# Gated linear attention: the short products of a head pair laid side by side in the array instead of padded with zeros

## The chip, the cores and the metric

One NeuronCore of a Trainium2 chip runs the whole program. The metric is the device time of one execution in microseconds (us). "PE" is TensorE, whose matmuls and weight loads ("PEld") the profile records apart; "DVE", "ACT" and "POOL" are the vector, scalar and GpSimd engines; "SP" issues most of the DMAs.

## The reference, cut to what matters

The program is one layer of a decoder trunk over 2048 tokens: an input projection, three token mixers in parallel (MLA, RWKV-7 and chunked gated linear attention, GLA), gates, and an output projection. The change touches GLA alone. It has 4 heads, keys of 64 and values of 128 channels, and for a chunk of tokens it computes, per head,

```python
def step(state, inp):
    q_t, k_t, v_t, b_t = inp                      # b: running sum of log decays in the chunk
    diff = b_t[:, :, None] - b_t[:, None, :]
    dec = jnp.exp(jnp.where(causal, diff, -jnp.inf))
    att = jnp.einsum('bihd,bjhd,bijhd->bhij', q_t, k_t, dec)
    o = (jnp.einsum('bhij,bjhv->bihv', att, v_t)
         + jnp.einsum('bihk,bhkv->bihv', q_t * jnp.exp(b_t), state))
    b_last = b_t[:, -1]
    state = (state * jnp.exp(b_last)[..., None]
             + jnp.einsum('bjhk,bjhv->bhkv', k_t * jnp.exp(b_last[:, None] - b_t), v_t))
    return state, o
```

## The kernel before

The phases follow each other: RWKV (with many of the projections), MLA, GLA, merge. PE is kept busy in RWKV and GLA by projections whose results are needed later. In GLA these are the gate columns: class `Gates` issues 108 units, each 8 groups of three 512-column matmuls (lines 133 to 135, output tile `psd`), with weights that SP loads as `w_raw`, ACT rounds to `w_hi` (line 118) and POOL completes to `w_lo` (line 119).

GLA works on 16 chunks of 128 tokens, numbered `g`. Four heads make two pairs, `p`; the two heads of a pair lie in partitions 0 to 63 and 64 to 127 of the same tiles. For a chunk there are three steps:

- `prepare(g)`: for each of six levels (64, 32, 16, 8, 4, 2 tokens) it makes a tile `qk` that holds decayed keys at the even halves of a level's blocks and decayed queries at the odd halves. DVE subtracts (line 1059, tile `e`), ACT takes the exponential, DVE multiplies the queries (line 1063, `qk<-e,q`) and POOL the keys. Line 1072 makes the queries of the last level, line 1073 the queries `qe` that meet the state. A query tile has two copies, one per head, and in each copy the other head's partitions are zero; so DVE works on 64 partitions at a time, twice. The zeros are written once, in the memsets of line 981.
- `scores(g)`: the products of queries and keys, per pair. The stationary operand is 128 partitions (both heads) by 64 or 32 tokens, the moving operand holds the two zero-padded copies side by side, and all go to one PSUM tile `psc` per pair: one 64-token product, two of 32 tokens from the second level, sixteen 32x32 blocks from the next four levels, and four from the plain keys `kx`. That is 23 products a pair, 46 a chunk, all on line 1086. DVE masks and adds them (lines 1099, 1101), POOL and ACT place the result in `a` (tile `ga`).
- `result(g)`: per pair and head, `qe` times the state (line 1117, `pso<-gs,qk`), plus `a` times the values (line 1120, `pso<-vt,ga`); then keys times values for the new state (line 1112, `pso<-vt,kt`), as one 128x256 product of which only the two diagonal blocks are used, and DVE updates the state (line 1124, tile `gs`).

All operands are fp32 here, and the profile records each such product as two LDWEIGHTS and two MATMULs. "128\*32" in a row is the size of the array's tile that the product uses, rows by columns.

Each engine runs its instructions in a fixed order. The program is written as one stream, and a scheduler interleaves it with its own estimates of durations; `ga.behind` also keeps a step's first product behind a given number of gate units. `ga.until` sets how many units are written between the steps. An engine that waits holds everything behind it.

Of the kernel before, what the change touches and what calls it, by code (L numbers as in the profile page):

```python
# [847 lines left out]
AHEAD = 1.5  # L848
# [98 lines left out]
def phase_gla(k, more, a_up, y_dram, x, w_gate, pre):  # L947
# [3 lines left out]
    with ExitStack() as st:  # L951
# [23 lines left out]

        QK = []
        for i in range(2):
            ts_ = [qkp[i].tile([128, 2, 2, 128], F32, name=f"qk{i}{n}") for n in range(len(LEVELS) + 1)]
            ts_.insert(-1, qkp[i].tile([128, 2, 2, 2, 128], F32, name=f"q{i}"))
            for n, t in enumerate(reversed(ts_)):  # L980
                (nc.vector, nc.gpsimd)[n % 2].memset(t, 0.0)
            QK.append(ts_)
        state, A = [], []
        for p in range(2):
            s_ = per.tile([128, 256], F32, name=f"gs{p}")
            nc.vector.memset(s_, 0.0)
            state.append(s_)
            for i in range(2):
                a = per.tile([128, 2, 128], F32, name=f"ga{p}{i}")
                nc.gpsimd.memset(a, 0.0)  # L990
                A.append(a)
        glam = k.c("glam", 192).rearrange("p (l t) -> p l t", t=32).unsqueeze(2).broadcast_to([128, 6, 2, 32])
        own = k.c("own32", 4).unsqueeze(2).broadcast_to([128, 4, 32])
# [50 lines left out]
        def prepare(g, kx, z, b, eb, kt, vt):  # L1044
# [5 lines left out]
            for hd, hs in heads:  # L1050
                nc.scalar.dma_start(out=q[hs, hd], in_=more[0:2, hs, g * 128:g * 128 + 128].rearrange("n p t -> p n t"))
            for s, o in zip(LEVELS, lv):
# [9 lines left out]
                for hd, hs in heads:  # L1062
                    nc.vector.tensor_tensor(out=v4(o[:, hd])[hs, :, 1, :], in0=ev[hs, :, 1, :],
                                            in1=v4(q[:, hd])[hs, :, 1, :], op=ALU.mult)
                nc.gpsimd.tensor_tensor(out=v4(o[:, 0])[:, :, 0, :], in0=ev[:, :, 0, :], in1=v4(kx)[:, :, 0, :],
# [5 lines left out]
            for hd, hs in heads:  # L1071
                nc.vector.tensor_tensor(out=odd(q1[:, hd])[hs], in0=e1[hs], in1=odd(q[:, hd])[hs], op=ALU.mult)
                nc.vector.tensor_tensor(out=qe[hs, hd], in0=eb[hs], in1=q[hs, hd], op=ALU.mult)

        def scores(g, kx, z, b, eb, kt, vt):
            c = g % 2
            *lv, q01, qe = QK[c]
            for p in range(2):
                a = A[2 * p + c]


                pc = ps_c[p].tile([128, 512], F32, name=f"psc{p}")
                pl = pc[:, 0:384].rearrange("p (l h t) -> p l h t", l=6, h=2)
                p64 = pc[0:64, 384:512].rearrange("p (h t) -> p h t", h=2)
                p32 = pc[:, 384:448].rearrange("p (h t) -> p h t", h=2)
                mm = lambda o, l, r: nc.tensor.matmul(o, lhsT=l, rhs=r, start=True, stop=True)
                m = mm(p64, lv[0][:, 0, p, 0:64], lv[0][:, :, p, 64:128])
                ga.behind(m, ga.done - AHEAD + p)
                mm(p32[96:128], lv[1][:, 0, p, 0:32], lv[1][:, :, p, 32:64])
                mm(p32[64:96], lv[1][:, 0, p, 64:96], lv[1][:, :, p, 96:128])  # L1090
                for i in range(5):
                    for j in range(4):
                        gs = slice(32 * j, 32 * j + 32)
                        if i < 4:
                            mm(pl[gs, i], lv[2 + i][:, 0, p, gs], lv[2 + i][:, :, p, gs])
                        else:
                            mm(pl[gs, 4:6], kx[:, c, p, gs], q01[:, :, :, p, gs])
                bm = t2.tile([128, 6, 2, 32], F32, name="bm")
                nc.vector.tensor_tensor(out=bm, in0=pl, in1=glam, op=ALU.mult)
# [479 lines left out]
```

## Time and profile before

| | |
|---|---|
| median of 3 runs | 3022.0 us (3018.12 to 3023.85) |
| the profiled execution | 3010.5 us, span 3008.7 us |
| PE busy | 2908.3 us, 97% of the span, 17728 matmul records |
| DVE / ACT / POOL busy | 59% / 50% / 49% |
| granted TensorE clock, mean | 0.989 |
| short products of GLA on PE | between 1853 and 2485 us of the span |

A PE that shows 97% busy is the engine to watch, but its records overlap: a matmul's duration covers the time until its result is out, while the next one starts earlier. What a product costs is therefore read from the distance between starts in the timeline. "Idle before, releaser" tells what an engine waited for.

### The profile page before, as it was taken

The page shows a single profiled execution, that of the slowest core. Times are in us where ns is not written, and L with a number is a line of the kernel's source. Part 1 is how long each engine was busy: PE and PEld are TensorE (multiplying, and loading weights), DVE is VectorE, ACT ScalarE, POOL GpSimd, SP SyncE. Part 2 cuts the span into 40 slices and gives each one's busy share as a digit, 9 for nine tenths or more (in the row PEclk, how much of TensorE's full clock was granted, in tenths as well). Part 3 has the DMA queues.
Part 4 walks back from the last instruction along what each step waited for, and adds up shares of the span by engine and source line. Part 5 has one row for each costly group of instructions (what it writes and reads, how often), then busy time and mean ns, then how long its engine had stood idle before and what let it go on. Part 6 is the DMA issues. An engine that isn't in the chain of part 4 may idle for free. (4 is left out here: it accounts for less than half of the span.)

```text
span 3008.7 us, 52742 instructions
## 1 busy us (share of the span) xinstructions
PE 2908.3 (97%) x17728; PEld 2395.9 (80%) x17728; DVE 1761.0 (59%) x4677; ACT 1503.9 (50%) x3463; POOL 1474.7 (49%) x1945
## 2 busy tenths in 40 slices
PE   7998999999999999999999999999999999999998
PEld 6776777777777878789999887788788888778887
DVE  3558675667746544388888886744324312975443
ACT  4444434454444436577877775554334434554221
POOL 4644544454444435555544555776334424575322
PEclk9999999999999999999999999999999999999999
DMA  4333323323233334300000014444223226866422
GB/s 135 105 100 103 90 85 101 93 77 86 78 106 86 106 112 144 113 20 22 19 20 16 15 62 148 148 143 136 92 96 101 92 91 203 288 201 212 137 97 78
DMA packets 285184, 312.67 MB, mean 104 GB/s; under 512 B 77920, under 2 KB 234608, under 8 KB 284912
## 3 DMA queue, kind: packets, MB, share of 16 engines
q1 hardware_dynamic: 259088, 278.76, 29.3%
q10 hardware_dynamic: 25824, 30.54, 3.1%
q8 instruction: 140, 2.29, 0.3%
q14 instruction: 132, 1.08, 0.1%
HBM read 233.16 MB, written 76.02 MB: 103 GB/s over the span
## 5 line engine op out<-in xcount | busy, mean ns | idle before, releaser
L119 POOL TENSOR_TENSOR w_lo<-w_raw,w_hi 128x256 fp32r<-128x256 f32 x848 | 645.0, 768 | 818.9 <-ACT w_hi L118 770.6
L133 PE MATMUL psd<-hh,w_hi 128*128 128x512 f32 x1952 | 795.1, 408 | 10.7 <-ACT w_hi L118 4.2
L135 PE MATMUL psd<-hh,w_lo 128*128 128x512 f32 x1952 | 788.4, 406 | 9.2 <-POOL w_lo L119 8.7
L134 PE MATMUL psd<-hl,w_hi 128*128 128x512 f32 x1952 | 778.3, 399 | 0.0
L118 ACT CAST w_hi<-w_raw 128x256 fp32r<-128x256 f32 x848 | 336.4, 404 | 501.8 <-PE psd L134 281.9
L135 PEld LDWEIGHTS psd<-hh,w_lo 128*128 128x128 f32 x1952 | 371.4, 190 | 95.5 <-POOL w_lo L119 17.9
L133 PEld LDWEIGHTS psd<-hh,w_hi 128*128 128x128 f32 x1952 | 371.2, 190 | 91.7 <-issue 8.9
L134 PEld LDWEIGHTS psd<-hl,w_hi 128*128 128x128 f32 x1952 | 371.1, 190 | 74.8 <-issue 1.2
L1286 POOL TENSOR_SCALAR P<-P,nm 128x1024 f32<-128x1024 f32 (+2 forms) x192 | 166.1, 875 | 192.5 <-DVE nm L1283 144.6
L1306 DVE TENSOR_TENSOR tl<-pst,th 128x512 fp32r<-128x512 f32 (+2 forms) x352 | 193.4, 562 | 33.6 <-ACT th L1305 32.0
L1305 ACT CAST th<-pst 128x512 fp32r<-128x512 f32 (+2 forms) x352 | 165.2, 488 | 81.6 <-PE pst L1301 42.5
L1278 ACT ACTIVATE P<-P,nm 128x1024 f32<-128x1024 f32 (+2 forms) x192 | 172.3, 901 | 14.8 <-DVE nm L1274 14.5
L1264 DVE TENSOR_SCALAR_CACHE_REDUCE P<-pss 128x512 f32<-128x512 f32 (+3 forms) x288 | 168.2, 593 | 13.1 <-PE pss L135 9.5
L1301 PE MATMUL pst<-cs,P 128*128 128x128 f32 x1088 | 166.0, 274 | 0.0
L1323 PE MATMUL pso<-th,v 128*128 128x256 f32 x576 | 150.9, 284 | 2.6 <-DVE yo L1331 2.6
L1323 PE MATMUL pso<-tl,v 128*64 128x256 f32 x576 | 139.9, 282 | 0.7 <-DVE tl L1306 0.7
L1301 PEld LDWEIGHTS pst<-cs,P 128*128 128x128 f32 x1088 | 125.6, 141 | 9.1 <-DVE tl L1306 0.4
L133 PE MATMUL pss<-kh,qh 128*128 128x512 f32 (+2 forms) x320 | 128.7, 402 | 0.6 <-DVE mx L1268 0.2
L119 POOL TENSOR_TENSOR wb_lo<-wb_raw,wb_hi 128x256 fp32r<-128x256 f32 x96 | 87.8, 921 | 80.6 <-ACT wb_hi L118 65.4
L1323 PEld LDWEIGHTS pso<-th,v 128*128 128x128 f32 x576 | 108.8, 189 | 11.8 <-DVE yo L1331 2.8
L135 PE MATMUL pss<-kh,ql 128*128 128x512 f32 (+2 forms) x320 | 116.4, 365 | 0.6 <-POOL ql L1244 0.6
L134 PE MATMUL pss<-kl,qh 128*128 128x512 f32 (+2 forms) x320 | 116.3, 364 | 0.0
(403 smaller groups left out, 5925.2 us busy)
## 6 DMA issues: line engine op xcount, KB each, us to landing
w_raw<-in_w_gate_dram SPq DMA_DIRECT2D x448, 128.0 KB, 2.2
pre<-plain SPq DMA_DIRECT2D x144, 256.0 KB, 2.3
w_raw<-in_w_rwkv_dram SPq DMA_DIRECT2D x208, 128.0 KB, 2.2
w_raw<-in_w_more_dram SPq DMA_DIRECT2D x192, 128.0 KB, 2.2
h_g<-pre SPq DMA_DIRECT2D x48, 512.0 KB, 4.4
h_x<-in_x_dram SPq DMA_DIRECT2D x44, 512.0 KB, 4.5
more<-plain SPq DMA_DIRECT2D x48, 256.0 KB, 2.7
wb_raw<-in_w_br_dram ACTq DMA_DIRECT2D x96, 128.0 KB, 3.5
```

What stands on the lines that cost most here:

```text
L118: nc.scalar.copy(hi, src)
L119: (sub or nc.gpsimd).tensor_tensor(out=lo, in0=src, in1=hi.bitcast(F32), op=ALU.subtract)
L133: mm(out, lhsT=lhs[0], rhs=rhs[0], start=start, stop=False)
L134: mm(out, lhsT=lhs[0], rhs=rhs[1], start=False, stop=False)
L135: m = mm(out, lhsT=lhs[1], rhs=rhs[0], start=False, stop=stop)
L1264: nc.vector.tensor_scalar(out=pt[:, c0:c0 + f], in0=s_[:, 0:f], scalar1=-MLA_SCALE, scalar2=3e38, op0=ALU.mult, op1=ALU.min, accum_out=mx[ ...
L1278: nc.scalar.activation(out=pt[:, cw], in_=pt[:, cw], func=AF.Exp, bias=nm[:, 0:1], scale=-1.0, accum_out=nm[:, 1 + n:2 + n])
L1286: nc.gpsimd.tensor_scalar(out=pt[:, cw], in0=pt[:, cw], scalar1=nm[:, 1:2], scalar2=1.0, op0=ALU.mult, op1=ALU.mult)
L1301: nc.tensor.transpose(tp[:, kl, qt, :], P[qt][:, kt * 128:(kt + 1) * 128], k.ident)
L1305: nc.scalar.copy(flat(th)[:, r], flat(tp)[:, r])
L1306: nc.vector.tensor_tensor(out=flat(tl)[:, r], in0=flat(tp)[:, r], in1=flat(th)[:, r].bitcast(F32), op=ALU.subtract)
L1323: nc.tensor.matmul(d_, lhsT=l_, rhs=r_, start=kt == 0 and j == 0, stop=last and kl == 1 and j == 1)
```

## The change

The zero-padded copies go. A query tile has one copy for both heads, `qk` is [128, 2, 128] instead of [128, 2, 2, 128], and DVE multiplies 128 partitions at once. In the scores each product is made per head, with 64 rows of the array each: the first head's in rows 0 to 63, the second's in rows 64 to 127, and each head has a PSUM bank of its own, `psc[hd]`, that now holds both pairs. So there are 92 products a chunk, and they stand in one run; masks and copies are made per head over both pairs. The products with the state are made per head with 64 rows as well, into `po[0]` and `po[1]`. The product for the new state is made per head with 64 columns of the array and all 128 rows; it goes to the second half of `po[0]`, and the state holds 128 instead of 256 columns. The memsets of the zeros go, except those of one query tile per buffer. The queries come in one DMA a chunk instead of two.

```diff
@@ phase_gla
-            ts_ = [qkp[i].tile([128, 2, 2, 128], F32, name=f"qk{i}{n}") for n in range(len(LEVELS) + 1)]
-            ts_.insert(-1, qkp[i].tile([128, 2, 2, 2, 128], F32, name=f"q{i}"))
-            for n, t in enumerate(reversed(ts_)):
-                (nc.vector, nc.gpsimd)[n % 2].memset(t, 0.0)
+            ts_ = [qkp[i].tile([128, 2, 128], F32, name=f"qk{i}{n}") for n in range(len(LEVELS) + 1)]
+            ts_.insert(-1, qkp[i].tile([128, 2, 2, 128], F32, name=f"q{i}"))
+            (nc.vector, nc.gpsimd)[i].memset(ts_[-2][:, 1], 0.0)
...
@@ prepare
-            for hd, hs in heads:
-                nc.scalar.dma_start(out=q[hs, hd], in_=more[0:2, hs, g * 128:g * 128 + 128].rearrange("n p t -> p n t"))
+            nc.scalar.dma_start(out=q, in_=more[0:2, :, g * 128:g * 128 + 128].rearrange("n p t -> p n t"))
...
-                for hd, hs in heads:
-                    nc.vector.tensor_tensor(out=v4(o[:, hd])[hs, :, 1, :], in0=ev[hs, :, 1, :],
-                                            in1=v4(q[:, hd])[hs, :, 1, :], op=ALU.mult)
+                nc.vector.tensor_tensor(out=v4(o)[:, :, 1, :], in0=ev[:, :, 1, :], in1=v4(q)[:, :, 1, :], op=ALU.mult)
...
-            for hd, hs in heads:
-                nc.vector.tensor_tensor(out=odd(q1[:, hd])[hs], in0=e1[hs], in1=odd(q[:, hd])[hs], op=ALU.mult)
-                nc.vector.tensor_tensor(out=qe[hs, hd], in0=eb[hs], in1=q[hs, hd], op=ALU.mult)
+            nc.vector.tensor_tensor(out=odd(q1), in0=e1, in1=odd(q), op=ALU.mult)
+            nc.vector.tensor_tensor(out=qe, in0=eb, in1=q, op=ALU.mult)
@@ scores
+            pc = [ps_c[hd].tile([128, 2, 256], F32, name=f"psc{hd}") for hd in range(2)]
+            def mm(at, out, l, r):
+                for hd, hs in heads:
+                    m = nc.tensor.matmul(out(pc[hd]), lhsT=l[hs], rhs=r[hs], start=True, stop=True)
+                    if at and hd == 0:
+                        ga.behind(m, ga.done - AHEAD)
             for p in range(2):
...
-                m = mm(p64, lv[0][:, 0, p, 0:64], lv[0][:, :, p, 64:128])
-                ga.behind(m, ga.done - AHEAD + p)
+                mm(p == 0, lambda o: o[0:64, p, 192:256], lv[0][:, p, 0:64], lv[0][:, p, 64:128])
...
-                            mm(pl[gs, i], lv[2 + i][:, 0, p, gs], lv[2 + i][:, :, p, gs])
+                            mm(False, lambda o: o[gs, p, 32 * i:32 * i + 32], lv[2 + i][:, p, gs], lv[2 + i][:, p, gs])
...
@@ result
+            po = [ps_o.tile([128, 512], F32, name="pso") for _ in range(2)]
+            a = A[c]
             for p in range(2):
-                for hd in range(2):
-                    m = nc.tensor.matmul(po[:, hd], lhsT=qe[:, hd, p], rhs=state[p][:, hd * 128:hd * 128 + 128], start=True, stop=False)
...
-                    nc.tensor.matmul(po[:, hd], lhsT=a[:, hd], rhs=vt[p][:, c, hd], start=False, stop=True)
-                nc.scalar.copy(osb[:, c, 2 * p:2 * p + 2], po)
-                pd_ = ps_o.tile([128, 256], F32, name="pso")
-                mm(pd_, kt[:, c, p], flat(vt[p][:, c]))
+                for hd, hs in heads:
+                    m = nc.tensor.matmul(po[hd][:, ps], lhsT=qe[hs, p], rhs=state[p][hs], start=True, stop=False)
...
+                for hd, hs in heads:
+                    nc.tensor.matmul(po[hd][:, ps], lhsT=a[:, hd, p], rhs=vt[p][:, c, hd], start=False, stop=True)
+            for p in range(2):
+                pd_ = po[0][:, 256 + 128 * p:384 + 128 * p]
+                for hd, hs in heads:
+                    nc.tensor.matmul(pd_[hs], lhsT=kt[:, c, p, hs], rhs=vt[p][:, c, hd], start=True, stop=True)
                 nc.vector.scalar_tensor_tensor(out=state[p], in0=state[p], scalar=eb[:, c, p, 127:128], in1=pd_,
                                                op0=ALU.mult, op1=ALU.add)
+            for hd in range(2):
+                nc.scalar.copy(osb[:, c, hd:4:2], po[hd][:, 0:256].rearrange("p (q t) -> p q t", q=2))
```

In the changed kernel the score products are on line 1080, the products with the state on 1115, `a` times values on 1119, and the new state's products on 1123. Three places show what the scheduler makes of it; a row is the line, the operation, output and inputs, and the output's partitions by columns ("x2": twice in a row).

On PE, the last chunk's `result` for the first pair, before (`psd` rows are gate products, on all of the array):

```order
L135 MATMUL psd_29709<-hh_25590,w_lo 128x512
L1117 MATMUL pso<-gs_22355,qk_22345 128x128
L1120 MATMUL pso<-vt_28327,ga_22359 128x128
L1117 MATMUL pso<-gs_22355,qk_22345 128x128
L1120 MATMUL pso<-vt_28327,ga_22359 128x128
L1112 MATMUL pso<-vt_28327,kt 128x256
L133 MATMUL psd_29819<-hh_23214,w_hi 128x512
```

The same place after the change, where both pairs' results now stand in one run:

```order
L135 MATMUL psd_30251<-hh_25773,w_lo 128x512
L1115 MATMUL pso<-gs_22341,qk_22338 128x128 x2
L1119 MATMUL pso<-vt_28720,ga_22347 128x128 x2
L1115 MATMUL pso<-gs_22343,qk_22338 128x128 x2
L1119 MATMUL pso<-vt_28721,ga_22347 128x128 x2
L1123 MATMUL pso<-vt_28720,kt 64x128 x2
L133 MATMUL psd_30361<-hh_23266,w_hi 128x512
```

Before, every product in this stretch uses all 128 rows and columns of the array; after, it goes from 128x128 to 64 rows, back, to 64 rows, back, to 64 columns and back to the gates, and the second pair's products for the state stand apart, 21 gate products later.

On PE, in the middle of the phase, where a block of the gates' input is turned, the score products of a chunk are interleaved with gate products. Before:

```order
L1086 MATMUL psc_26211<-qk_22343 32x64 x4
L133 MATMUL psd_26035<-hh_25584,w_hi 128x512
L1086 MATMUL psc_26211<-qk_22344 32x64
L133 MATMUL psd_26155<-hh_23222,w_hi 128x512
L134 MATMUL psd_26155<-hl_23223,w_hi 128x512
L1086 MATMUL psc_26211<-qk_22344 32x64 x3
```

After:

```order
L1080 MATMUL psc_26430<-qk_22336 32x32
L1080 MATMUL psc_26429<-qk_22336 32x32
L133 MATMUL psd_26373<-hh_23278,w_hi 128x512
L134 MATMUL psd_26373<-hl_23279,w_hi 128x512
L1080 MATMUL psc_26430<-qk_22336 32x32
L1080 MATMUL psc_26429<-qk_22336 32x32
```

Such places are more frequent now: counted over the whole phase, the score products stand in 36 unbroken runs before and in 53 after.

On DVE, near the end of MLA, the zeros of the first buffer before:

```order
L1268 ISA mx 128x1
L981 MEMSET qk_22329 128x512
L981 MEMSET qk_22328 128x512
L981 MEMSET qk_22326 128x512
L981 MEMSET qk_22324 128x512
L1331 TENSOR_TENSOR yo<-pso,yl 64x256
L1306 TENSOR_TENSOR tl<-pst,th 128x512
```

And after:

```order
L1270 ISA mx 128x1
L979 MEMSET q_22330 128x256
L1276 TENSOR_REDUCE nm<-mx 128x1
L1333 TENSOR_TENSOR yo<-pso,yl 64x256
L1308 TENSOR_TENSOR tl<-pst,th 128x512
L202 TENSOR_SCALAR h_x<-h_x,rs 128x1024
```

Four memsets of 512 columns have become one of 256 ahead of MLA's own work.

More of the change, by code (lines that the diff above doesn't have):

```diff
@@ L984, in phase_gla @@
         for p in range(2):
-            s_ = per.tile([128, 256], F32, name=f"gs{p}")
+            s_ = per.tile([128, 128], F32, name=f"gs{p}")
             nc.vector.memset(s_, 0.0)
             state.append(s_)
[L988 to L993, printed above, removed]
+        for i in range(2):
+            a = per.tile([128, 2, 2, 128], F32, name=f"ga{i}")
+            nc.gpsimd.memset(a, 0.0)
+            A.append(a)
+        glam = k.c("glam", 192).rearrange("p (l t) -> p l t", t=32).unsqueeze(1).broadcast_to([128, 2, 6, 32])
+        own = k.c("own32", 4).unsqueeze(1).unsqueeze(3).broadcast_to([128, 2, 4, 32])
         flat = lambda a: a.rearrange("p a b -> p (a b)")
@@ L1061, in prepare @@
                 nc.scalar.activation(out=e, in_=e, func=AF.Exp, scale=1.0 / 16)
[L1062 to L1065 removed]
+                nc.vector.tensor_tensor(out=v4(o)[:, :, 1, :], in0=ev[:, :, 1, :], in1=v4(q)[:, :, 1, :], op=ALU.mult)
+                nc.gpsimd.tensor_tensor(out=v4(o)[:, :, 0, :], in0=ev[:, :, 0, :], in1=v4(kx)[:, :, 0, :],
                                         op=ALU.mult)
@@ L1111, in result @@
             qe = QK[c][-1]
-            mm = lambda o, l, r: nc.tensor.matmul(o, lhsT=l, rhs=r, start=True, stop=True)
+            po = [ps_o.tile([128, 512], F32, name="pso") for _ in range(2)]
+            a = A[c]
             for p in range(2):
-                a = A[2 * p + c]
-                po = ps_o.tile([128, 2, 128], F32, name="pso")
-                for hd in range(2):
-                    m = nc.tensor.matmul(po[:, hd], lhsT=qe[:, hd, p], rhs=state[p][:, hd * 128:hd * 128 + 128], start=True, stop=False)
-                    if hd == 0:
-                        ga.behind(m, ga.done - AHEAD + p)
-                    nc.tensor.matmul(po[:, hd], lhsT=a[:, hd], rhs=vt[p][:, c, hd], start=False, stop=True)
-                nc.scalar.copy(osb[:, c, 2 * p:2 * p + 2], po)
-                pd_ = ps_o.tile([128, 256], F32, name="pso")
-                mm(pd_, kt[:, c, p], flat(vt[p][:, c]))
+                ps = slice(128 * p, 128 * p + 128)
+                for hd, hs in heads:
+                    m = nc.tensor.matmul(po[hd][:, ps], lhsT=qe[hs, p], rhs=state[p][hs], start=True, stop=False)
+                    if hd == p == 0:
+                        ga.behind(m, ga.done - AHEAD)
+                for hd, hs in heads:
[4 more added lines that the diff above has]
+                    nc.tensor.matmul(pd_[hs], lhsT=kt[:, c, p, hs], rhs=vt[p][:, c, hd], start=True, stop=True)
                 nc.vector.scalar_tensor_tensor(out=state[p], in0=state[p], scalar=eb[:, c, p, 127:128], in1=pd_,
                                                op0=ALU.mult, op1=ALU.add)
+            for hd in range(2):
+                nc.scalar.copy(osb[:, c, hd:4:2], po[hd][:, 0:256].rearrange("p (q t) -> p q t", q=2))
         def finish(B, osb):
```

29 lines of the change are left out of this document (12 added, 17 removed).

## The prediction

> **What bounds the kernel now.** I read the page's first part first (PE is busy nearly all of the span), then the stretches of GLA, then what PE waited for, then the timeline of PE at one chunk. In the stretches each engine's figure is its busy time:
>
> ```profile
> 1780.00:1800.00 20.00, 17.40 (x118) 16.01 (x117) 17.40 (x47) 14.06 (x31) 12.52 (x15) 0.91 0.47 163
> 1850.00:1880.00 30.00, 25.43 (x190) 19.40 (x188) 26.89 (x54) 16.68 (x45) 22.68 (x41) 0.89 0.33 108
> 1890.00:1910.00 20.00, 16.05 (x79) 12.74 (x79) 19.40 (x43) 11.63 (x32) 16.09 (x31) 0.91 0.40 138
> 2200.00:2460.00 260.00, 260.00 (x1781) 212.64 (x1781) 84.01 (x197) 95.75 (x241) 106.09 (x169) 1.00 0.28 93
> ```
>
> The columns are PE, PEld, DVE, ACT, POOL, then the granted clock. From 2200 to 2460 PE never pauses and DVE, ACT and POOL are busy a third of the time: there, time is PE's starts alone, and work taken from the others is worth nothing. Around 1790 and from 1850 to 1910 it is different: PE pauses, DVE is nearly full, and the clock is below 1. What PE waited for between 1780 and 1910 (total, times, longest):
>
> ```profile
> PE pst L1040 <- ACT kt L1041: 3.0, 1, 3.0
> PE psc L1086 <- DVE qk L1063: 2.9, 4, 1.2
> PE pso L1323 <- DVE yo L1331: 2.6, 1, 2.6
> PE pso L1117 <- DVE qk L1073: 1.7, 1, 1.7
> PE pso L1112 <- DVE gs L1124: 0.8, 1, 0.8
> ```
>
> So two prices decide: what the short products cost on PE in 16 chunks, and how much of these pauses at the start goes.
>
> **Score products, per chunk.** The last chunk's scores stand in one run; the starts are in the first column:
>
> ```profile
> 2453.47 0.39 PE L135 MATMUL psd<-hh,w_lo 128*128 128x512 f32 x1
> 2453.79 1.06 PE L1086 MATMUL psc<-qk 128*64 128x128 f32 x36
> 2454.64 0.28 PE L1086 MATMUL psc<-q,kx 128*32 128x128 f32 x2
> ...
> 2455.06 1.06 PE L1086 MATMUL psc<-qk 128*64 128x128 f32 x36
> ...
> 2456.32 0.50 PE L133 MATMUL psd<-hh,w_hi 128*128 128x512 f32 x1
> 2456.66 0.40 PE L134 MATMUL psd<-hl,w_hi 128*128 128x512 f32 x1
> ```
>
> 2.53 us for 46 products, and a frame: the gate product ahead holds PE 0.32 us and the one behind 0.34, where 0.23 is the usual distance (2478.01 to 2478.24 below). Together 2.73 us. Two other stretches give the parts:
>
> ```profile
> 1880.69 0.38 PE L1086 MATMUL psc<-q,kx 128*32 128x128 f32 x4
> 1881.00 0.49 PE L1117 MATMUL pso<-gs,qk 128*128 128x128 f32 x2
> 1881.32 0.39 PE L1120 MATMUL pso<-vt,ga 128*128 128x128 f32 x2
> 1881.55 0.39 PE L1117 MATMUL pso<-gs,qk 128*128 128x128 f32 x2
> ...
> 1882.42 0.43 PE L1086 MATMUL psc<-qk 128*64 128x128 f32 x2
> 1882.79 0.70 PE L1112 MATMUL pso<-vt,kt 128*128 128x256 f32 x2
> ```
>
> A 128x128 product in a steady row costs 0.22 us (1881.32 to 1881.55), but 0.32 directly behind a tile of another size (1881.00): 0.10 more, to load weights. The 64-column product costs 0.37 until another size follows: a record lasts some 0.28 (0.39 less the 0.11 between the two records of a product), so its second record starts 0.43 - 0.28 = 0.15 behind its first, 0.05 late, and some 0.20 more pass before another size may start. So of the 0.85 us to the first `kx` product, 0.49 is left for 34 records on four column tiles: 14 ns a record, 29 ns a product. Where nothing holds them, records start closer: these rows count score records in flight within 16, 37, 96 and 117 ns (PE, then PEld), and after 37 ns four matmuls run, after 96 ns eight loads are out:
>
> ```profile
> 1883.40:1883.42 0.02, 0.00 (x1) 0.00 (x1) 0.00 (x0) 0.00 (x0) 1.00 0.00 0
> 1883.40:1883.44 0.04, 0.02 (x4) 0.02 (x4) 0.00 (x0) 0.00 (x0) 1.00 0.00 0
> 1883.40:1883.50 0.10, 0.08 (x5) 0.08 (x8) 0.00 (x0) 0.00 (x0) 1.00 0.08 11
> ```
>
> That is three starts in 21 ns, 7 ns each. After the change each record streams half the columns on one of eight tiles. I take 7 ns, the row with nothing in the way; the other end is the 14 ns of now. The row-wise halving has a price that the RWKV phase shows, where 64\*64 and 128\*64 products (64 columns moved) alternate, and where the second kind stands alone:
>
> ```profile
> 374.74 0.33 PE L547 MATMUL psu<-uv,mr 128*64 128x64 f32 x2
> 375.00 0.33 PE L515 MATMUL psq<-uv,ma 64*64 64x64 f32 x2
> 375.25 0.33 PE L547 MATMUL psu<-uv,mr 128*64 128x64 f32 x2
> 217.32 0.68 PE L547 MATMUL psu<-uv,mr 128*64 128x64 f32 x8
> 217.93 0.71 PE L575 MATMUL psz<-uv,bkt 128*128 128x128 f32 x4
> ```
>
> Alternating, a product (two records) takes 0.26 us. Eight records alone take 0.61, of which entering and leaving is some 0.14: 0.12 a product. So a change of rows alone, with the columns kept, costs 0.14 us.
>
> After, per pair: the 64-token products of both heads 0.26 (the rows above, the second head's some 0.01 behind the first's); then 88 records (44 products) x 7 ns = 0.62, plus 0.15 until another size may follow: 0.77. Twice 1.03 and the frame of 0.20: 2.26 against 2.73. **Sixteen chunks: -7.5 us.** At 14 ns it would be +12.
>
> **Products of the result, per chunk.** Steady, before:
>
> ```profile
> 2478.01 0.39 PE L135 MATMUL psd<-hh,w_lo 128*128 128x512 f32 x1
> 2478.24 0.38 PE L1117 MATMUL pso<-gs,qk 128*128 128x128 f32 x2
> ...
> 2479.12 0.60 PE L1112 MATMUL pso<-vt,kt 128*128 128x256 f32 x2
> 2479.37 0.59 PE L133 MATMUL psd<-hh,w_hi 128*128 128x512 f32 x1
> 2479.80 0.40 PE L134 MATMUL psd<-hl,w_hi 128*128 128x512 f32 x1
> ```
>
> No size changes here. Four products take 0.88; the last one and the first gate product 0.68, less 0.23 for the gate product itself, 0.45. So 1.33 a pair, 2.66 a chunk. After: entering costs 0.09. The two 64-row products with the state run together: the second records 0.21 behind the first (0.11, and 0.10 for a load of 128 columns), 0.01 for the second head, then 0.20 until another size may follow, 0.42. The two with `a`: records 0.21, 0.11 and 0.11 apart, then 0.20, 0.64 in place of 0.44. Both again: 0.42 + 0.64. The state's pair in 64 columns: 0.37, and the gate product behind 0.11 more. Then, 21 gate products later, 0.09 + 0.37 + 0.11. Sum 3.26 against 2.66: the halved streams are paid back by six changes of size. **Sixteen chunks: +9.7 us** (if the row change were free, -3).
>
> [...]
>
> **Broken runs.** 53 runs of score products instead of 36. Each has the frame of 0.20 and the 0.15 at its end: 17 x 0.33 = 5.6, and a few state products that the scheduler set apart in the first chunks, 4 x 0.33. **+7 us.** PE in all: **+9.2 us.**
>
> **The start.** DVE's zeros stand ahead of what MLA waits for:
>
> ```profile
> 1785.97 2.11 DVE L981 MEMSET qk<- 128x512 f32 x4
> 1788.00 0.35 DVE L1331 TENSOR_TENSOR yo<-pso,yl 64x256 f32<-64x256 f32 x1
> 1788.41 0.38 PE L1323 MATMUL pso<-th,v 128*128 128x256 f32 x1 [2.60 <-DVE yo L1331]
> ```
>
> One memset of half the width, 0.27 us, replaces these: **-1.8 us** of 2.6 (0 if another wait is next, as `tl` behind `yo` on DVE may be). Then DVE between 1850 and 1910:
>
> ```profile
> L1063 DVE TENSOR_TENSOR qk<-e,q 64x128 f32<-64x128 f32 x46 | 21.1, 458 | 0.7
> L1059 DVE TENSOR_TENSOR e<-b 128x128 f32<-128x128 f32 x24 | 11.1, 500 | 0.2
> L1073 DVE TENSOR_TENSOR qk<-eb,q 64x256 f32<-64x256 f32 x8 | 5.3, 661 | 0.1
> ```
>
> Lines 1063 and 1073 keep their columns and halve their count. At 500 ns, the row of the same form on 128 partitions, 23 take 11.5 us, and 4 take 2.6: 12 us less in 60 that DVE all but fills. The other four waits of the list are 8.4 us and all end with DVE or with ACT behind it. The first of them come when only some 4 us are saved, so I take **-6 us** (bounds 0 and -8.4). The clock stood at 0.91, 0.89 and 0.91 over 20, 30 and 20 us, 6.9 us lost, in and just behind the pauses; half of it: **-3.4 us** (bounds 0 and -6.9). The start: -11.2.
>
> **At nothing.** The state update on half the columns, fewer POOL instructions for `ga`, one DMA of queries instead of two and the copies per head lie beside a PE that is full (2200 to 2460); without that cover they would be worth at most what DVE saves. A wait is added: the second pair's product for the state follows DVE's update of the first, since both lie in `po[0]`. Behind it wait gate products; 21 of them, 4.8 us, stand in between, so it costs nothing except in the first chunks, up to 2 us. Masks now begin only after both pairs' products, but 72 or more gate products, 16 us, follow.
>
> **Sum.** +9.2 - 11.2 = -2.0 us. The profiled execution took 3010.5 us (span 3008.7), so 3008.5; it stands 11.5 below the median of the runs, 3022.0, and against that I say 3020. A measurement of this kernel tells 0.2%, some 6 us, from no change.
>
> **Rivals.**
> - *Only the start counts* (faster): all of the pauses and of the clock's loss go, 17.9 instead of 11.2: 3013. DVE's 12 us speak for it; against it, that PE's order sets the GLA steps earlier where DVE is expected to be faster, and waits anew.
> - *The change of rows is free* (faster): result products -3 instead of +9.7, so 3007. The alternating rows at 374.74 speak against it; no row has 64 rows with 128 columns. Decides if 64-row products start 0.22 us behind a gate product's start. [...]
> - *Issue bounds the scores* (slower): a product cannot be sent faster than the 29 ns of now, so twice the products take twice as long: 44 x 29 = 1.28 instead of 0.62, twice a chunk, +21: 3041. For it, no row shows more than a burst at 7 ns; against it, at 29 ns four tiles are full with their columns, which explains it without any limit. It decides above some 11 ns a record. [...]
> - *The second head does not run beside the first* (slower; the change doesn't do what it says): every 64-row pair is serial, 0.22 x 32 for the state, 0.12 x 32 for the 64-token products, some 0.15 x 32 for the rest: +16, 3036. No row has two 64-row products on one set of columns.
>
> **Chances.** No measurable change 0.42 (own range 3014 to 3028), only the start 0.18, free change of rows 0.12, issue 0.16, serial heads 0.12. Faster 0.30, same 0.42, slower 0.28. The range 3006 to 3041 leaves out about half of the last cases' outer sides, under 2 in 10.
>
> **What would show it.** Right: in a late chunk the score run takes 2.1 to 2.3 us and the result's two stretches 3.1 to 3.4 without their 21 gate products; 64-row products show 0.2 us ahead of each change; the wait for `yo` near 1788 is under 1 us, those for `qk` under 3. Wrong: score records 12 ns or more apart on average, state pairs 0.2 us apart within the pair, or new waits of PE on DVE behind `po`.

## The result, and the profile after

The changed kernel takes 3036.4 us, the median of 7 runs (3032.07 to 3042.7), against 3018.12 for the kernel before on the same chip (7 runs, 3011.11 to 3023.85). The ratio is 1.0061 with an interval of 1.0045 to 1.0077: **18 us slower**. Forecast were 3020 and no measurable change.

The profiled execution of the changed kernel is the longest of its seven (3042.7 us, span 3040.9, mean clock 0.985). It is 32 us longer than the profiled one of before, but 14.6 us of that lie ahead of MLA, where both do the same work in the same order: MLA's first transposition starts at 1280.2 us before and at 1294.8 after, and in the fourteen traces of this study it lies between 1276 and 1295. So spans are not compared below. What is compared is the stretch from that transposition to GLA's last one, with each 512-column product of lines 133 to 135 in it (3747 before, 3749 after) taken out at 0.2391 us (the mean distance between the starts of gate products in GLA before, 545.1 us for 2280), since the order moves gate products into and out of it. That stretch is 13.2 us longer after the change.

The start came out much as forecast. These are the stretches again (PE, PEld, DVE, ACT, POOL, granted clock), and PE's waits between 1780 and 1910 us:

```profile
1780.00:1800.00 20.00, 20.00 (x131) 17.69 (x131) 18.40 (x70) 15.28 (x35) 8.33 (x11) 1.00 0.26 77
1850.00:1880.00 30.00, 27.36 (x290) 20.71 (x289) 23.46 (x39) 17.91 (x46) 26.84 (x43) 0.94 0.41 128
1890.00:1910.00 20.00, 18.99 (x120) 15.33 (x121) 11.09 (x23) 12.88 (x34) 13.63 (x25) 0.91 0.40 125
2200.00:2460.00 260.00, 256.94 (x2234) 205.05 (x2233) 71.51 (x162) 95.14 (x240) 102.02 (x158) 1.00 0.28 92
```

```profile
PE pst L1038 <- ACT kt L1039: 2.1, 1, 2.1
PE pst L1012 <- ACT vt L1039: 1.3, 1, 1.3
PE pso L1115 <- DVE qk L1067: 0.8, 1, 0.8
PE pso L1325 <- DVE yo L1333: 0.8, 1, 0.8
...
PE psc L1080 <- DVE qk L1059: 0.3, 2, 0.2
```

The five waits of before were 11.0 us, these five are 5.3, and the wait for `yo` is 0.8 in place of 2.6. The clock lost 6.9 us in the three early stretches, now 3.6 (0.06 x 30 and 0.09 x 20). But the last row is new: from 2200 to 2460, where PE never paused before, it now stands still for 3 us. The list of waits behind 1910 us says where most of it is; its first row has no counterpart before:

```profile
PE psc L1080 <- issue: 5.9, 5, 1.9
```

Inside score runs PE pauses five times, and no engine, DMA or semaphore releases it ("issue"). The last chunk's run shows one of them; starts are in the first column:

```profile
2477.21 0.39 PE L135 MATMUL psd<-hh,w_lo 128*128 128x512 f32 x1
2477.53 1.05 PE L1080 MATMUL psc<-qk 64*64 64x64 f32 x74
...
2478.73 1.05 PE L1080 MATMUL psc<-qk 64*64 64x64 f32 x74
...
2479.62 0.34 PE L1080 MATMUL psc<-q,kx 64*32 64x64 f32 x10
2481.72 0.30 PE L1080 MATMUL psc<-q,kx 64*32 64x64 f32 x4 [1.75 <-issue]
...
2483.00 0.59 PE L134 MATMUL psd<-hl,w_hi 128*128 128x512 f32 x1
2483.38 0.63 PE L135 MATMUL psd<-hh,w_lo 128*128 128x512 f32 x1
2483.81 0.63 PE L133 MATMUL psd<-hh,w_hi 128*128 128x512 f32 x1
```

The run of 92 products has started all but two of them by 2479.75. Then nothing starts for 1.97 us. And 1.3 us behind the pause the gate products take 0.59 and 0.63 in place of 0.39, and start 0.38 and 0.43 us apart: the clock has halved. Two of the pauses, with what follows them (the columns are those of the stretches):

```profile
2479.75:2481.72 1.97, 0.22 (x19) 0.05 (x7) 0.00 (x0) 0.00 (x0) 0.00 (x0) 1.00 0.31 99
2483.00:2486.40 3.40, 3.40 (x10) 2.66 (x9) 1.91 (x3) 1.20 (x6) 1.23 (x2) 0.50 0.00 0
2100.70:2102.70 2.00, 0.12 (x15) 0.01 (x1) 0.00 (x0) 0.58 (x2) 1.20 (x1) 1.00 0.36 121
2104.30:2107.60 3.30, 3.30 (x10) 2.51 (x10) 3.30 (x7) 1.93 (x5) 2.62 (x6) 0.51 0.15 39
```

What goes with the ends of these pauses is found in the third part of the page, the DMA queues. Queue q8 carries instructions; that they are PE's is read from the number of its packets, which goes with the number of PE's records. The rows are those of before, of after, and of the kernel below that makes every score product twice (packets, MB, share):

```profile
q8 instruction: 140, 2.29, 0.3%
q8 instruction: 152, 2.49, 0.4%
q8 instruction: 175, 2.87, 0.4%
```

Each packet is 16 KB. Before, 140 packets serve 35456 records of PE (17728 matmuls and as many loads), after 152 serve 38528, and the third kernel's 175 serve 44416: one for every 253 records or so. Taken one by one from the trace, each of the five pauses ended 1.1 to 1.5 us after one of these packets had landed, although the packets come some 15 us apart there. For the pause above the packet started at 2479.21 and took 1.41 us, and PE went on 1.1 us later.

The result step did what the prediction wrote. Again the starts, in a late chunk:

```profile
2422.12 0.39 PE L135 MATMUL psd<-hh,w_lo 128*128 128x512 f32 x1
2422.44 0.49 PE L1115 MATMUL pso<-gs,qk 64*128 64x128 f32 x4
2422.86 0.71 PE L1119 MATMUL pso<-vt,ga 128*128 128x128 f32 x4
2423.50 0.49 PE L1115 MATMUL pso<-gs,qk 64*128 64x128 f32 x4
2423.93 0.71 PE L1119 MATMUL pso<-vt,ga 128*128 128x128 f32 x4
2424.57 0.44 PE L1123 MATMUL pso<-vt,kt 128*64 128x128 f32 x4
2424.94 0.50 PE L133 MATMUL psd<-hh,w_hi 128*128 128x512 f32 x1
```

The distances are 0.42, 0.64, 0.43, 0.64 and 0.37: the terms 0.42, 0.64, 0.42, 0.64 and 0.37.

### The profile page after: what moved, and what is told of

The parts are those of the page before. It is cut to its first block, busy times and chain, and to the rows that moved or that the text cites. A ratio compares the mean times of both kernels' runs of the same rounds, so it can differ in the third digit from the quotient of the medians.

```text
span 3040.9 us, 55541 instructions
## 1 busy us (share of the span) xinstructions
PE 2934.6 (97%) x19264; PEld 2399.5 (79%) x19264; DVE 1711.0 (56%) x4542; ACT 1505.4 (50%) x3463; POOL 1461.9 (48%) x1904
## 4 chain that ended last, share of the span: by engine, by line
PE 77%; DVE 11%; DMA 5%; issue 3%; POOL 2%; ACT 2%; SPq 0%; ACTq 0%; POOLq 0%; DVEq 0%
PE psd L133 12%; PE psd L135 12%; PE psd L134 12%; PE pso L1325 4%; PE pst L1303 4%; PE pss L133 3%; PE pss L135 3%; PE pss L134 3%; DVE xt L454 2%; DVE xtmp L452 2%; PE psb L135 2%; PE psg L134 2%; PE psg L135 2%; PE psg L133 2%; PE psb L133 2%
## 5 line engine op out<-in xcount | busy, mean ns | idle before, releaser
L133 PEld LDWEIGHTS psd<-hh,w_hi 128*128 128x128 f32 x1952 | 372.5, 191 | 95.6 <-ACT w_hi L118 12.6
L1280 ACT ACTIVATE P<-P,nm 128x1024 f32<-128x1024 f32 (+2 forms) x192 | 172.3, 902 | 12.0 <-DVE nm L1276 11.7
```

The costliest lines, as they stand in the source:

```text
L133: mm(out, lhsT=lhs[0], rhs=rhs[0], start=start, stop=False)
L1280: nc.scalar.activation(out=pt[:, cw], in_=pt[:, cw], func=AF.Exp, bias=nm[:, 0:1], scale=-1.0, accum_out=nm[:, 1 + n:2 + n])
```

## The experiments

Each kernel was timed beside the kernel before on the same chip. Two columns make the verdicts: the time against before, and the stretch from MLA to the end of GLA as defined above (327.4 us before). "Result" and "scores" are sums of the distances between starts of these products in GLA; pauses and waits behind such a product are inside.

| kernel | ratio to before (interval) | us against before | stretch against before | scores | result |
|---|---|---|---|---|---|
| before | | | | 47.7 | 40.2 |
| changed | 1.0061 (1.0045 to 1.0077) | +18.4 | +13.2 | 57.3 | 47.5 |
| pairs apart | 1.0024 (1.0014 to 1.0034) | +7.2 | +4.6 | 46.8 | 54.9 |
| result on the full array | 1.0006 (0.9994 to 1.0017) | +1.8 | +0.6 | 54.7 | 37.4 |
| both | 0.9987 (0.9975 to 1.0000) | -3.9 | -3.9 | 48.3 | 38.2 |
| DVE's work back | 1.0133 (1.0116 to 1.0149) | +40.1 | +38.5 | 61.6 | 54.2 |
| both, 32-column tiles | 0.9974 (0.9961 to 0.9987) | -7.8 | -10.7 | 43.1 | 37.7 |
| before, 32-column tiles | 0.9948 (0.9934 to 0.9962) | -15.7 | -11.0 | 38.0 | 38.8 |
| scores twice | 1.0369 (1.0353 to 1.0384) | +111 | +107 | 134.0 | 46.8 |
| one head | 0.9980 (0.9970 to 0.9991) | -6.0 | -2.6 | 28.4 | 55.6 |
| grouped result | 0.9969 (0.9957 to 0.9981) | -9.4 | -13.0 | 45.1 | 37.8 |
| rows, then columns | 0.9960 (0.9946 to 0.9973) | -12.1 | -13.6 | 40.1 | 38.8 |
| grouped, 32-column tiles | 0.9954 (0.9940 to 0.9967) | -13.9 | -14.0 | 42.6 | 38.9 |
| columns, grouped result | 0.9967 (0.9956 to 0.9978) | -10.0 | -12.7 | 38.8 | 44.3 |

(The us against before are the ratio less one, times 3018.5.)

**Pairs apart.** The second pair's score products are written behind some gate units:

```diff
             for p in range(2):
-                mm(p == 0, lambda o: o[0:64, p, 192:256], ...)
+                if p:
+                    between()      # ga.until((LEAD + (g + 0.4) * STEP) / 108, turn)
+                mm(True, lambda o: o[0:64, p, 192:256], ...)
```

> The second pair's 46 score products of a chunk are written after some gate units, so that PE gets 46 in a row and not 92; each product stays as in the changed kernel. Theory 1 (PE runs out of instructions): in the changed kernel PE stands still for 1.7 to 2.1 us inside four long score runs, and each time a 16 KB packet of PE's instructions had landed 1.1 to 1.5 us before it went on; 92 products are some 23 KB of instructions in 2.4 us. With 46 in a row and gate products between, no stall over 1 us is left inside a late run; that is worth some 11 us, of which some 16 more runs with a frame of 0.2 and an end of 0.15 take 6 back: 5 us less than the changed kernel, about 13 above the kernel before. Theory 2 (the stall is a wait for something in the run itself, a PSUM bank or the second head's tile): the stalls stay and the frames come on top, 6 us more than the changed kernel, 24 above before.

Measured: 7 us above before, 11 less than the changed kernel. No pause over 0.4 us is left between two score records anywhere, no "issue" row is left in the list of waits behind 1910 us, and the clock stays at full speed from 1105 us to the end:

```profile
1850.00:1880.00 30.00, 26.36 (x310) 19.83 (x309) 25.62 (x45) 20.70 (x55) 27.76 (x47) 1.00 0.39 125
1890.00:1910.00 20.00, 20.00 (x185) 15.79 (x183) 7.71 (x13) 8.93 (x24) 11.31 (x18) 1.00 0.78 237
2200.00:2460.00 260.00, 259.94 (x2332) 207.62 (x2331) 65.71 (x166) 94.19 (x242) 110.14 (x164) 1.00 0.29 92
```

Theory 1 holds, and the edit is worth more than the 5 us expected. The expectation gave 11 us for the pauses and took 6 back for 16 more runs; but the score runs stayed at 53, and the two early stretches at half clock went as well (1.00 in both first rows, in place of 0.94 and 0.91). It had a side effect: the scheduler now set the two heads' state products apart from each other, and the result's groups rose from 47.5 to 54.9 us.

**Scores twice.** The test from the other side, a run of 184 products:

```diff
-            for p in range(2):
-                mm(p == 0, lambda o: o[0:64, p, 192:256], ...)
+            for rnd, p in ((0, 0), (0, 1), (1, 0), (1, 1)):
+                mm(rnd == p == 0, lambda o: o[0:64, p, 192:256], ...)
```

> The changed kernel, but every score product is made twice into the same place, so a chunk has 184 in a row. Theory 1 (PE runs out of instructions): 64 products, or 16 KB of instructions, come at best every 2.1 to 2.9 us (a packet's 1.0 to 1.4 us and 1.1 to 1.5 more until PE goes on), so 92 more products take 3.0 to 4.2 us, and nearly every run of 184 has one or two stalls: 48 to 67 us more than the changed kernel, 66 to 85 above the kernel before. Theory 2 (the stalls are no matter of the run's length): 92 more products at the 22 ns of an undisturbed run take 2.0 us, 32 us more than the changed kernel, 50 above before, with as many stalls as it had.

Measured: 111 us above before, 93 above the changed kernel. Both expectations fall short, theory 1 on the right side. The score groups rose by 76.7 us, 4.8 a chunk, and the waits behind 1910 us begin with

```profile
PE psc L1080 <- issue: 28.9, 19, 2.5
```

The trace has 21 pauses of 0.75 to 2.7 us between score records. Every one of them ended 1.20 to 1.51 us after a 16 KB packet of PE's instructions had landed. Behind most of them the clock was halved for 3.4 or 6.8 us: 25 such windows of 3.4 us between 1860 and 2570 us, against four there in the changed kernel. At half the speed these 21 more windows lose some 36 us, 14 of them inside the score groups; theory 1 had left that out. Taken together with the pairs apart: pauses appear where runs are long and go where they are short, and each ends behind a packet of instructions. That PE runs out of instructions there is the author's reading of this; how PE fetches them is not shown. By the count above, one packet comes for some 253 records: the changed run of 92 fp32 products is 368 records, more than one packet, the run of 46 is 184.

**Result on the full array.** One copy of the queries, zeros kept off the state's diagonal blocks, products as before:

```diff
-                for hd, hs in heads:
-                    m = nc.tensor.matmul(po[hd][:, ps], lhsT=qe[hs, p], rhs=state[p][hs], start=True, stop=False)
...
+                for hd in range(2):
+                    m = nc.tensor.matmul(po[:, hd], lhsT=qe[:, p], rhs=state[p][:, 128 * hd:128 * hd + 128], ...)
+                    nc.tensor.matmul(po[:, hd], lhsT=a[:, hd, p], rhs=vt[p][:, c, hd], start=False, stop=True)
...
+                nc.tensor.matmul(pd_, lhsT=kt[:, c, p], rhs=flat(vt[p][:, c]), start=True, stop=True)
+                for hd, hs in heads:   # the diagonal blocks alone
+                    nc.vector.scalar_tensor_tensor(out=state[p][hs, w], ...)
```

> Only the result step is undone: the queries for the state keep one copy, the state has 256 columns with zeros off its diagonal blocks, and all result products use 128 rows and 128 columns as in the kernel before; DVE updates the state in two halves. Scores as in the changed kernel. Theory 1 (changes of the tile's size cost what the timeline shows): the groups of the result lose the 7.4 us that they gained, and their frames some 2 more: 8 to 10 us less than the changed kernel, about 9 above the kernel before. Theory 2 (the result step is free and the stalls in the scores are all of the loss): within 3 us of the changed kernel, 15 to 21 above before.

Measured: 2 us above before, 17 less than the changed kernel, of which the result's groups are 10.1 (47.5 to 37.4). That is theory 1, with a larger effect than the 8 to 10 us expected; by the intervals the difference is 11 to 22 us. The stretch fell by 12.6: the result's groups and 2.6 us of the score groups. What the other 4 us of the time are, the trace does not show. Four pauses in score runs are left (0.4 to 2.5 us), as expected of an edit that leaves the runs alone.

**Both edits.**

> Both edits together: result products on the full array, and the scores' pairs apart. If both first theories hold, their gains add up: 5 and 9 us, so 14 less than the changed kernel, 4 above the kernel before, within what can be told from it. If the stalls are no matter of instructions, 3 us less than the changed kernel; if the result step is free, 5 less.

Measured: 4 us below before, 22 below the changed kernel; 14 were expected. Alone the two edits gained 11 and 17 us; within the intervals they add up.

**Grouped result.** If a change of tile size is what costs, the same 64-row and 64-column products in an order with fewer changes should be cheap:

```diff
+            with_state(0, True)       # the first pair's qe x state, both heads, opens the bank
+            with_values(0, False)
+            with_values(1, True)      # a x values of the second pair opens its columns
+            with_state(1, False)
...
-                pd_ = po[0][:, 256 + 128 * p:384 + 128 * p]
+                pd_ = po[p][:, 256:384]
```

A dependency without a semaphore holds the products in this order.

> The kernel with the pairs apart, but the result's products of a chunk are held in one order: the first pair's with the state, both pairs' with a, the second pair's with the state, both pairs' keys times values; the second pair's state product goes to the other bank. The same products on the same tiles with fewer changes of size. In the kernel with the pairs apart the three groups of the result take 54.9 us between the first and last step of GLA (22.6 with a, 20.0 with the state, 12.3 for the new state), in the changed kernel 47.5, in the one before 40.2. Theory 1 (a change of size is what costs): they fall to 42 to 44, 11 us less than the kernel with the pairs apart, some 4 below the kernel before. Theory 2 (products on half the rows or columns cost as much as on the whole, whatever stands beside them): they fall to 47.5 at best, 7 us less, level with the kernel before.

Measured: 9 us below before, 17 less than the kernel with the pairs apart. A late chunk:

```profile
2405.05 0.83 PE L1131 MATMUL pso<-vt,ga 128*128 128x128 f32 x6
2405.81 0.49 PE L1124 MATMUL pso<-gs,qk 64*128 64x128 f32 x4
2406.23 0.66 PE L1140 MATMUL pso<-vt,kt 128*64 128x128 f32 x8
2406.82 0.50 PE L135 MATMUL psd<-hh,w_lo 128*128 128x512 f32 x1
```

Both pairs' products for the new state take 0.59 us together, where one pair alone took 0.37 in the changed kernel, and they come straight behind the state products. The groups sum to 37.8 us: less than the 42 to 44 expected. That is no gain over the full array, though: the 40.2 of before hold 2.3 us of waits behind these products, and a late chunk's groups take 2.33 us here, 2.27 before, 2.86 in the changed kernel and 3.38 with the pairs apart. So the changes of size were the loss, and without most of them the halved products cost what the whole ones did.

**One head.** Of each pair only the first head's scores are made (the edit is `for hd, hs in heads[:1]`).

> The kernel with the pairs apart, but the score products of the second head of each pair are left out (the second head takes the first one's), so a pair has 23 products on 64 of the 128 rows. Theory 1 (the pace of a run is set by sending products, some 17 ns each, whatever tile they go to): a pair's run falls from 1.20 to 1.28 us to some 0.8, 32 times: 13 us less than the kernel with the pairs apart, 6 below the kernel before. Theory 2 (the pace is set by how long each tile of the array is held, and the heads' tiles run side by side): the run stays at 1.1 to 1.3 us, within 4 us of the kernel with the pairs apart, 3 to 7 above before.

Measured: 6 us below before, 13 less than with the pairs apart. That is to the microsecond what theory 1 said, which is luck in part: in the traces the score groups fell by 18.4 us and the stretch by 7.2. The argument rests on the runs themselves. A pair's run, first with both heads and then with one, each with the gate product ahead and the product behind:

```profile
2449.56 0.39 PE L135 MATMUL psd<-hh,w_lo 128*128 128x512 f32 x1
2449.88 1.05 PE L1080 MATMUL psc<-qk 64*64 64x64 f32 x74
...
2451.07 0.49 PE L1117 MATMUL pso<-gs,qk 64*128 64x128 f32 x4
```

```profile
2458.25 0.39 PE L135 MATMUL psd<-hh,w_lo 128*128 128x512 f32 x1
2458.57 0.75 PE L1080 MATMUL psc<-qk 64*64 64x64 f32 x36
...
2459.40 0.50 PE L133 MATMUL psd<-hh,w_hi 128*128 128x512 f32 x1
```

1.19 us against 0.83: the second head's 23 products cost 16 ns each although their rows of the array are free. So short score products gain next to nothing from standing side by side: the two heads share the sending of products.

**32-column tiles.** The prediction read 0.37 us for a 64-column product among 32-column ones. Two products of 32 columns do the same, once on the kernel before and once on the kernel with both edits:

```diff
-                m = mm(p64, lv[0][:, 0, p, 0:64], lv[0][:, :, p, 64:128])
+                for j in range(2):
+                    gs = slice(32 * j, 32 * j + 32)
+                    m = mm(p64[gs], lv[0][:, 0, p, gs], lv[0][:, :, p, 64:128])
```

> The kernel before, unchanged but for its 64-token product, which is made as two products of 32 key tokens each (128 rows, 32 columns). Theory 1 (the change of columns costs 0.37 us a pair, as the rows of the last chunk show): two products of 29 ns take its place, 0.31 us less, 32 times: 10 us below the kernel before. Theory 2 (the 0.37 us belongs to the first product of any run): 0 to 2 us above before.

> As the kernel with the result on the full array and the pairs apart, but the 64-token product of a head is made as two products of 32 key tokens, so that all score products use tiles of 64 rows and 32 columns and no size changes inside a run. Theory 1 (the 0.26 us that a pair spends on its 64-token products is the change from 64 to 32 columns): a pair's 46 products become 48, and its run falls from 1.20 to 1.28 us to 1.0 to 1.1; 32 runs, 6 us less than without it, about 10 below the kernel before. Theory 2 (the 0.26 us belongs to the first products of any run behind a gate product): the runs get longer by 4 records, 0.03 us, and the time stays within 2 us of the kernel without it.

Measured: the kernel before gains 16 us. The other one gains 4 (its groups of scores 5.2, against 6 expected), which by the intervals alone could be nothing. A chunk's scores in the first:

```profile
2441.54 0.39 PE L135 MATMUL psd<-hh,w_lo 128*128 128x512 f32 x1
2441.86 0.80 PE L1086 MATMUL psc<-qk 128*32 128x128 f32 x38
...
2442.69 0.85 PE L1086 MATMUL psc<-qk 128*32 128x64 f32 x38
...
2443.75 0.50 PE L133 MATMUL psd<-hh,w_hi 128*128 128x512 f32 x1
```

1.89 us in place of 2.53, which is 0.64 for an expected 0.62. The interval of the time (11 to 20 us) has the expected 10 just outside; the groups fell by 9.7. Without a single row-wise product this kernel has the lowest ratio of all.

**DVE's work back.** The changed kernel, with DVE and POOL doing what they did before: the zeros are written at the old size again, and DVE multiplies by halves:

```diff
-                nc.vector.tensor_tensor(out=v4(o)[:, :, 1, :], in0=ev[:, :, 1, :], in1=v4(q)[:, :, 1, :], op=ALU.mult)
+                for hd, hs in heads:
+                    nc.vector.tensor_tensor(out=v4(o)[hs, :, 1, :], in0=ev[hs, :, 1, :], in1=v4(q)[hs, :, 1, :], op=ALU.mult)
```

> PE's products as in the changed kernel, but DVE's and POOL's work at the start is given back: the zeros are written over tiles of the old size (the second half of each is not read), and DVE multiplies each level's queries in two halves of 64 partitions, at the same columns. Theory 1 (the start gains what the waits show): the wait for yo near the first memset comes back to some 2.5 us, and PE's waits for qk with their lower clock: 8 to 11 us more than the changed kernel, 26 to 29 above the kernel before. Theory 2 (the lighter start was worth nothing, the order took its place): within 3 us of the changed kernel.

Measured: 40 us above before, 22 above the changed kernel, twice what theory 1 said. PE's waits between 1780 and 2560 us now have

```profile
PE pso L1127 <- DVE gs L1128: 5.8, 3, 3.4
...
PE pso L1329 <- DVE yo L1337: 2.6, 1, 2.6
```

and the stretch where the clock stood at 0.91 has 0.83:

```profile
1890.00:1910.00 20.00, 16.57 (x209) 12.79 (x196) 19.40 (x47) 8.39 (x26) 14.30 (x27) 0.83 0.15 46
```

The wait for `gs` is the second pair's product behind the state update in `po[0]`, which the prediction put at up to 2 us in the first chunks: with a slower DVE it is 5.8. Ten windows of 3.4 us at half clock in GLA, against four, are 10 us more. So with the changed kernel's products and their new wait, the lighter work of DVE and POOL is worth 22 us, not 11.

**Rows, then columns.** The first two chunks' scores by rows, the rest as before with 32-column tiles; the zeros are written later:

```diff
+            rows = g < 2
...
+                if g < 4:
+                    for n, t in enumerate((q01, *lv)):
+                        (nc.vector, nc.gpsimd)[n % 2].memset(t, 0.0)
```

> The first two chunks' scores by rows as in the changed kernel (with 32-column tiles alone and the pairs apart), all later chunks as in the kernel before with its 64-token product made as two of 32 tokens; the result on the full array for all chunks, with one copy of its queries and zeros off the state's diagonal blocks. So DVE has the light work while PE waits for it at the start, the zeros are written in front of the third and fourth chunk, and PE has the cheaper products from there on. Theory 1 (the gain at the start and the gain of 32-column tiles are independent): the 16 us of the kernel with 32-column tiles alone, and 7 to 9 at the start (0.8 in place of 2.6 us of wait for yo, 4 fewer of the waits, 3 of the clock), less 2 for two chunks with more runs: 20 to 24 below the kernel before. Theory 2 (the lighter start gains nothing by itself, since the order puts the steps earlier): 14 to 17 below before.

Measured: 12 below before (8 to 16), no better than the 32-column tiles alone. That is nearest to theory 2, and the trace (of the longest of its eight executions) shows a reason: the waits of the start come back with the third chunk's preparation. DVE's rows, then PE's:

```profile
1886.71 6.62 DVE L1074 TENSOR_TENSOR qk<-e,q 64x128 f32<-64x128 f32 x10 [0.32 <-ACT e L1072]
1893.36 0.35 DVE L1185 SCALAR_TENSOR_TENSOR gs<-gs,eb,pso 64x128 f32<-64x128 f32 x1
```

```profile
1893.76 0.80 PE L1175 MATMUL pso<-gs,qk 128*128 128x128 f32 x2 [4.33 <-DVE gs L1185]
```

Ten multiplications by halves stand ahead of the state update in DVE's queue, and PE waits 4.3 us for the update. The clock halves there too: just behind the wait a 128x128 product starts every 0.43 us, in place of 0.22.

**The two combinations.** The grouped result with 32-column tiles by rows, and with the scores of before by columns:

> The kernel with the grouped result, with each head's 64-token product made as two products of 32 key tokens. So it is the changed kernel with none of its three costs: no run of 92, few changes of size in the result, none in the scores. Theory 1 (these gains add up): the grouped result stood 10.6 us below the kernel before, the 32-column tiles brought 3.9 in the other pair of kernels (5 in the groups of the trace): 14 to 17 below before. Theory 2 (the 3.9 was chance, the interval reaches to zero): 9 to 12 below.

> Scores as in the kernel before with 32-column tiles alone (zero-padded queries, 128 rows, one run a chunk), the result as in the kernel with the grouped result (one copy of its queries, half the state, few changes of size). It has the two halves of the case that were each the cheaper. Theory 1 (they add up): 15.7 us for the scores, 2.4 for the result's groups (37.8 us in place of 40.2): 17 to 20 below the kernel before. Theory 2 (the order that groups the products brings new waits for the state, since its update now stands behind everything): 10 to 14 below.

Measured: 14 and 10 us below before. The first is at the lower end of theory 1 (14 to 17); it is the change without its three costs. The second does not add up: its result groups take 44.3 us in place of 37.8. Theory 2 has the number (10 to 14), but not the reason: PE waits for no product of the result there. Of the 44.3, 2.2 us are one product of the gates' input that stands behind a state product and waits for DVE; a late chunk takes 2.52 us without any wait, in place of 2.33, and the early chunks' groups are torn apart by transpositions and gate products. The intervals of both overlap with that of the kernel before with 32-column tiles (11 to 20 us below), which remains the simplest of the faster ones.

## Why the prediction was wrong

**The score products (-7.5 us): the term that failed.** It took 7 ns a record, from a burst of four. In a run without a pause a pair takes 1.20 us, not 1.03, and nearly all of a chunk (176 and 182 of its 184 records) 2.43 and 2.48 us, not 2.06, against 2.53 before: some -1.3 us for sixteen chunks. In the run at 2449.88 the 7 ns last for some thirty records; then two records start every 17 ns. The rival that sending bounds the scores had the mechanism right, as the kernel with one head shows, and the price wrong: 16 ns a product (8 ns a record), not 29. The 29 were the array's, as the prediction argued: on four column tiles four records start every 56 ns in the kernel before, and every 32 with one head and half the columns. At 8 ns sending takes over, and twice the records at 8 ns are no cheaper than the old ones at 14.

**What no step had: instructions.** The prediction counted a run by its records' starts and "both pairs in one run" as a saving of frames. That the run doubles PE's records in the same 2.5 us (368 for 184, where one packet comes for some 253), and that PE may then wait for instructions, is in no term and no rival. In the changed kernel's trace it costs 5.9 us of pauses and, behind two of them, 3.4 us of half clock (two windows of 3.41 us, half lost); taking the runs apart gave 11 us back.

**Broken runs (+7): too high.** There are 53 runs as counted, but the stretches of gate products in GLA did not become more (96 before, 94 after), since score runs now often stand beside other short products. What is left are the ends, 17 x 0.15 = 2.6 us. As a check, the score groups of all chunks, without waits, pauses and time lost at half clock, are 43.6 us before and 46.1 after: +2.5 for this term and the first together, against -1.3 + 2.6 from single rows.

**The result (+9.7): right.** The groups rose by 7.4 us; those of before hold 2.3 us of waits, so the products alone cost 9.9 more. They lose 10.1 when they go back to the full array. The rivals of free rows and of a second head that runs alone fall here with the same rows: 0.42 and 0.64 us as worked out; and in the grouped kernel the second head's first record starts 7 ns behind the first's in the chunk shown. Among the short score products the second head does add its own time, 0.36 us a pair, but by its sending. That the changes of size are the price, the grouped kernel shows: the same products in an order with fewer changes take 37.8 us instead of 54.9.

**The start (-11.2): nearly right.** Waits fell by 5.7 us (7.8 forecast), the clock's loss by 3.3 (3.4 forecast). The second pair's wait for the state update, which was put at nothing, does not show in the changed kernel. The rival that only the start counts falls: the start gains its 9 us, and PE's costs are larger.

**The sum.** +2.5 for the score groups, +9.3 for instructions, +9.9 for the result, -9.0 for the start, and -1.0 for PE's other waits behind 1910 us (4.3 before, 3.3 after) make +11.7. The traces' stretch says +13.2, and the times say +18 (14 to 23). So the terms account for the stretch but for 1.5 us; some 5 us of the times (by the interval 0 to 10) lie outside it, and where is not shown. That 3036 is also the time of the rival in which the second head does not run beside the first is chance: in the result, which was nearly half of that rival's sum, the two heads do run side by side.

## What to carry to other kernels

Cutting a product into halves that can run side by side brought PE nothing here, once for the scores, where sending became the limit (16 ns a product), and once for the result, where changes of tile size did (9.9 us); what the change gained came from DVE's and POOL's lighter work at the start (9.0 us). Count records, instructions and changes of tile size, not columns. A long run of short fp32 products can leave PE standing until a packet of instructions has landed (5.9 us in the changed kernel, 28.9 with the scores made twice); put long products between such runs, keep them at the 46 to 48 products that had no such pause here, and look for waits that end with "issue". One mixed size in a run (a 64-column tile among 32-column ones) can cost as much as the change that one has in mind: without it the kernel before was 15.7 us faster, and the whole change cost 18.4.

## What the runs showed of the hardware

- PE's instructions come in packets of 16 KB, one for some 253 records. Each of 26 pauses in two kernels ended 1.1 to 1.5 us after one of them had landed. Runs of up to 48 fp32 score products had no such pause, chunks with runs of up to 92 had one in 5 of 16 (the changed kernel), and with runs of up to 184 in 15 of 16 (scores twice).
- A pause of 2 us can cost nearly as much again: behind the pauses at 2100.6 and 2479.8 us the clock was halved for 3.4 us. Behind one of 1.7 us (2234.4) it was not.
- Short fp32 products on separate tiles (most with 32 columns moved) were sent every 16 to 17 ns after a first burst, also the second head's, whose rows were free; long ones (128 columns moved) of two heads ran side by side, the second 7 ns behind the first.
- A 64-column product among 32-column ones cost some 0.3 us more than two 32-column products: 0.64 us a chunk, for two of them (2.53 against 1.89).
